# First MLP product: weights' high half with one 512-column moving operand instead of two of 256

## The chip, the cores and the metric

The kernel runs on one core of one Trainium2 chip. The metric is the device time of one execution in microseconds. Three runs of the kernel before have a median of 1898.04 us (1896.63 to 1898.8).

## What is computed

The reference is one layer of an encoder on x of 512 tokens by 2048 features, all in float32: a Conformer convolution module, then a squared-ReLU MLP, then a last RMSNorm.

```
h = rmsnorm(x, norm1_g)
u = h @ w_in + b_in;  val, gate = split(u)
u = causal_dwconv(val * sigmoid(gate), dw) + dw_b        # 31 taps
x = x + silu(layernorm(u, ln_g, ln_b)) @ w_out + b_out
x = x + square(relu(rmsnorm(x, norm2_g) @ mlp_w1)) @ mlp_w2   # 2048 -> 8192 -> 2048
out = rmsnorm(x, final_g)
```

## The kernel before

**Precision.** A float32 operand is kept as a high half (rounded to the matmul's fp32r type) and a low half (what is left). A product of two such operands is three matmuls into one PSUM tile: high by high, high by low, low by high. The helper `mm3` (L346 to L351) issues them: L349 multiplies the weights' high half wh with the input's high half, L350 wh with the input's low half, L351 the weights' low half wl with the input's high half. In the program's names the stationary operand (lhsT) is the weight, the moving one (rhs) the input.

**Stages.** First the convolution module runs, with its input product (to about 380 us) and its output product (L727 and L918, to about 590 us). Then comes the first MLP product, which is the stage that the change touches: a loop over 32 pairs of column blocks of mlp_w1 (`for n in range(NPAIR)`), from about 591 to 1247 us. Then comes the second MLP product (function `seven`) and the last norm.

**The first MLP product.** Each pair is a 2 by 2 block product by a scheme of seven products instead of eight, in the order FIRST: P1, P5, P6, P2, P7, P3, P4. An input factor of product x and row block p is the tile `y[p, x]`, 512 columns wide: its columns 0 to 255 (`t[:, :HT]`, HT = 256) are the high half of 256 tokens, columns 256 to 511 the low half. For each of the 8 row blocks p the loop calls `mm3`: three matmuls of 256 columns, 24 for a product, 168 for a pair, 5376 in all, all into the first 256 columns of a PSUM bank.

**Banks.** Four PSUM banks serve the loop. P1, P6, P7 and P4 accumulate one on the other in bank X, which alternates between two banks from pair to pair; P5 and P3 in bank Y; P2 in bank Z. After its last matmul each product's bank is read into a 256-column block of the pair's tile `four` (`READS`): P1, P5 and P6 by a ScalarE copy (L1037), P4 by a ScalarE relu (L1039), P2, P7 and P3 by a VectorE add to a block that an earlier product has filled (L1041). A product that goes on in a bank waits until the product before it there has been read.

**What runs beside it.** The weights of a product are made three products ahead (`stream.AHEAD = 3`, class `Early`): block differences on VectorE (L223), the cast to the high half on ScalarE (L212, L217), the low half on VectorE (L218) or GpSimd (L213). The pair before goes through class `Squares`, one step behind each product: relu (L964, three of the four blocks), square (L967), the high half (L973), sums and low halves on GpSimd (L978 to L981, L993), and stores to the buffer `spill` in memory, which the second product fetches (L953). The program is written out by hand here (`manual_schedule`): each engine works its instructions off in the order in which the code issues them. In the first pair the loop also holds the last of the residual (L868 to L873) and the last input factors y (L861, L862).

Of the kernel before, what the change touches and what calls it, by code (L numbers as in the profile page):

```python
# [14 lines left out]
AF = mybir.ActivationFunctionType  # L15
ALU = mybir.AluOpType
PSUM = bass.MemoryType.PSUM

P = 128
# [50 lines left out]
OPENS = ("P1", "P5", "P2")  # L70
# [14 lines left out]
HT = T // 2  # L85
# [3 lines left out]
def trunk(ctx: ExitStack, tc: tile.TileContext, xT, vec, fg, w_in, w_out, w1s, w2s, w2b, out):  # L89
    nc = tc.nc  # L90
# [21 lines left out]
    def bank(tag="mm"):  # L112
        return (psm if tag == "mm" else psx).tile([P, 512], F32, tag=tag, name=tag)
# [172 lines left out]
    def chunk():  # L286
        got = stream.get(cursor[0])
        cursor[0] += 1
        return got
# [56 lines left out]
    def mm3(ps, w, x, first, last, **how):  # L346

        (wh, wl), (xh, xl) = w, x
        nc.tensor.matmul(out=ps, lhsT=wh, rhs=xh, start=first, stop=False, **how)  # L349
        nc.tensor.matmul(out=ps, lhsT=wh, rhs=xl, start=False, stop=False, **how)  # L350
        nc.tensor.matmul(out=ps, lhsT=wl, rhs=xh, start=False, stop=last, **how)  # L351
# [6 lines left out]
    h = [None] * NT  # L358
# [494 lines left out]
    def pieces(p, products):  # L853
        for x in products:
            pool, tag, n = HOME[x]
            t = pool.tile([P, T], F32R, tag=tag, name="y", bufs=n)
            if x in ("P1", "P2", "P4"):
                f = parts[2 * p + (x != "P1")][:, first if x == "P4" else second]
            else:
                f = parts["s", p][{"P5": "s1", "P6": "s2", "P7": "s3", "P3": "s4"}[x]]  # L860
            nc.scalar.copy(out=t[:, :HT], in_=f)  # L861
            nc.vector.tensor_tensor(out=t[:, HT:], in0=f, in1=t[:, :HT].bitcast(F32), op=sub)  # L862
            y[p, x] = t

    def residual(n, b, pt):

        for i in range(4):
            nc.tensor.transpose(out=pt[:, i * P : (i + 1) * P], in_=xt[4 * n + i][:, b * P : (b + 1) * P], identity=ident)  # L868
        x2 = early.tile([P, 512], F32, tag="t", name="x2", bufs=4)
        nc.scalar.copy(out=x2, in_=pt)  # L870
        nc.scalar.dma_start(out=acc[b][n], in_=x2)
        sq = early.tile([P, 512], F32, tag="t", name="sq", bufs=4)
        nc.scalar.activation(out=sq, in_=pt, func=AF.Square, accum_out=ss[:, 4 * b + n : 4 * b + n + 1])  # L873
# [21 lines left out]
    with tc.manual_schedule():  # L895
        for n in range(4):
            evacuate(n, ps[n])
        for q in range(1, 4):
            ps = [bank() for _ in range(4)]
            stream.AHEAD = 3 if q < 3 else 2  # L900
            for c in range(8 if q < 3 else 6):
                w = chunk()
# [10 lines left out]
        for n in range(4):  # L913
            for k in range(12, NT):
                wh, wl = (x[:, k % 2 * 512 + n * P :][:, :P] for x in ends[k // 2 - 6])
# [31 lines left out]
        def fetch(n, sl=slice(0, 7 * HT)):  # L947

            i = n % SLOTS
            if n not in pairs:  # L950
                pairs[n] = tuple(slots[i].tile([P, 7 * HT], F32R, tag=f"{x}{i}", name=x, bufs=1) for x in ("ah", "al"))
            for h in range(2):
                nc.sync.dma_start(out=pairs[n][h][:, sl].bitcast(F32), in_=spill[n][:, h, sl])  # L953

        class Squares:
# [5 lines left out]
                self.block = dict(zip(("21", "11", "22", "12"), (self.a[:, i * HT : (i + 1) * HT] for i in range(4))))  # L961

            def relu(self):
                nc.scalar.activation(out=self.a[:, HT:], in_=self.a[:, HT:], func=AF.Relu)  # L964

            def square(self):
                nc.scalar.activation(out=self.a, in_=self.a, func=AF.Square)  # L967
# [53 lines left out]
        banks = {x: bank() for x in "0YZ1"}  # L1021
        before = None
        for n in range(NPAIR):
            now = None
            for i, product in enumerate(FIRST):
                w = chunk()
                where = {"X": str(n % 2)}.get(BANK[product], BANK[product])
                x = banks[where][:, :HT]
                for p in range(8):
                    t = y[p, product]  # L1030
                    sl = slice(p * P, (p + 1) * P)
                    mm3(x, tuple(h[:, sl] for h in w), (t[:, :HT], t[:, HT:]), product in OPENS and p == 0, p == 7, skip_group_check=True)
                if now is None:
                    now = Squares(n)
                to = now.block[READS[product]]
                if product in ("P1", "P5", "P6"):
                    nc.scalar.copy(out=to, in_=x)  # L1037
                elif product == "P4":
                    nc.scalar.activation(out=to, in_=x, func=AF.Relu)  # L1039
                else:  # L1040
                    nc.vector.tensor_tensor(out=to, in0=x, in1=to, op=ALU.add)  # L1041
                if before:
                    before.step(i)
                if n == 0:
                    if i < 2:
                        residual(3, 2 * i, banks["1"])
                        residual(3, 2 * i + 1, banks["Z"])
                    elif i == 2:
                        pieces(6, ("P7", "P3"))
                        pieces(7, ("P7", "P3"))  # L1050
                        gone.close()
                        stage = gone.enter_context(tc.tile_pool(name="stage", bufs=1, side="right", reuse_waits="tile"))
                    elif i == 3:
                        nc.vector.tensor_reduce(out=r2, in_=ss.rearrange("p (b n) -> p b n", n=4), axis=mybir.AxisListType.X, op=ALU.add)
                        nc.vector.tensor_scalar(out=r2, in0=r2, scalar1=1.0 / D, scalar2=RMS_EPS, op0=ALU.mult, op1=ALU.add)
                        nc.vector.reciprocal(out=r2, in_=r2)
                if n == NPAIR - 1:
                    if i == 3:
                        left.close()
                        slots += [ctx.enter_context(tc.tile_pool(name="slots", bufs=1, reuse_waits="tile"))] * 2  # L1060
                        slots += [late.enter_context(tc.tile_pool(name="slots2", bufs=1, reuse_waits="tile"))] * 2
                        for p in range(4):
                            fetch(p, slice(0, FORE))
                    elif i > 4:
                        for p in (2 * i - 10, 2 * i - 9):
                            fetch(p, slice(FORE, 7 * HT))
            before = now
# [72 lines left out]
    for q in range(2):  # L1140
        seven(NG - 1, q, 1)
        last_pair(LASTS + q)
        for n in (2 * q, 2 * q + 1):
            for m in range(4):
                raw = wts.tile([P, 1024], F32, tag="raw", name="raw", bufs=4)
                nc.sync.dma_start(out=raw[:, :512], in_=w2b[n, m])
                wh = lasts.tile([P, 512], F32R, tag=f"wh{n}{m}", name="w2h")
                wl = lasts.tile([P, 512], F32R, tag=f"wl{n}{m}", name="w2l")
# [6 lines left out]
    for i in range(2):  # L1155
        t = wts.tile([P, 1024], F32, tag="raw", name="fgt", bufs=4)
        nc.scalar.dma_start(out=t, in_=fg[i * 1024 : (i + 1) * 1024].partition_broadcast(P))
        fgt += [t[:, :512], t[:, 512:]]
    for b in range(NTOK):
# [6 lines left out]
        for i, cs in enumerate(pieces):  # L1166
# [3 lines left out]
            for kk in range(4):  # L1170
                ak = a[kk]
                wh, wl = wl2[kk][n]
# [64 lines left out]
```

## Time and profile before

| what | value |
|---|---|
| median of three runs | 1898.04 us |
| profiled execution | 1898.16 us |
| its span on the core | 1896.4 us |
| granted TensorE clock, mean | 0.988 |
| TensorE busy | 1838.8 us (97%) |
| VectorE / ScalarE / GpSimd busy | 1254.5 / 1138.0 / 1247.4 us |
| matmuls | 10866 |
| read from memory, written | 255.65 MB, 65.54 MB |

The engines carry short names in the profile: PE is TensorE's matmuls, PEld its weight loads, DVE VectorE, ACT ScalarE, POOL GpSimd, SP the queue that issues most loads. L349 is line 349 of the kernel. The matmuls of TensorE are pipelined: the duration in a row is longer than the time from one start to the next. The busy time of an engine counts no time twice.

### The profile page before, as it was taken

The page shows a single profiled execution, that of the slowest core. Times are in us where ns is not written, and L with a number is a line of the kernel's source. Part 1 is how long each engine was busy: PE and PEld are TensorE (multiplying, and loading weights), DVE is VectorE, ACT ScalarE, POOL GpSimd, SP SyncE. Part 2 cuts the span into 40 slices and gives each one's busy share as a digit, 9 for nine tenths or more (in the row PEclk, how much of TensorE's full clock was granted, in tenths as well). Part 3 has the DMA queues.
Part 4 walks back from the last instruction along what each step waited for, and adds up shares of the span by engine and source line. Part 5 has one row for each costly group of instructions (what it writes and reads, how often), then busy time and mean ns, then how long its engine had stood idle before and what let it go on. Part 6 is the DMA issues. An engine that isn't in the chain of part 4 may idle for free.

```text
span 1896.4 us, 29173 instructions
## 1 busy us (share of the span) xinstructions
PE 1838.8 (97%) x10866; PEld 1634.9 (86%) x10866; DVE 1254.5 (66%) x1997; ACT 1138.0 (60%) x1770; POOL 1247.4 (66%) x704
## 2 busy tenths in 40 slices
PE   6999999989998999999999999979999999999998
PEld 5888888978887999999999999957888888888876
DVE  8899999994338655555555555526666666666685
ACT  6444444456346666666666666646767776777663
POOL 5699999944433667767767767666566556665643
PEclk9999999999999999999999999989999999999999
DMA  5233333206333455655655655587746647556342
GB/s 213 91 97 96 100 122 100 78 1 220 114 121 122 161 198 186 210 194 181 216 193 179 221 193 179 198 319 275 277 134 232 235 148 271 187 172 237 99 145 100
DMA packets 93165, 323.08 MB, mean 170 GB/s; under 512 B 10336, under 2 KB 10976, under 8 KB 93024
## 3 DMA queue, kind: packets, MB, share of 16 engines
q1 hardware_dynamic: 72432, 258.76, 41.8%
q10 hardware_dynamic: 20592, 62.46, 8.2%
q8 instruction: 85, 1.39, 0.3%
q14 instruction: 56, 0.46, 0.1%
HBM read 255.65 MB, written 65.54 MB: 169 GB/s over the span
## 4 chain that ended last, share of the span: by engine, by line
PE 84%; DVE 7%; DMA 2%; ACT 2%; POOL 2%; issue 1%; SPq 0%; ACTq 0%; DVEq 0%; POOLq 0%
PE mm L350 26%; PE mm L351 26%; PE mm L349 26%; PE mm L727 7%; DVE ax L432 1%; POOL b L166 1%; POOL wl L187 1%; DMA xt<-in_xT 1%; DVE d L616 1%; DVE xl L343 1%; ACT ax L191 0%; DVE y L862 0%; DMA spill<-sl 0%; DVE d L694 0%; DMA acc<-x 0%
## 5 line engine op out<-in xcount | busy, mean ns | idle before, releaser
L349 PE MATMUL mm<-y,wh 128*128 128x256 f32 x1792 | 508.1, 284 | 2.6 <-ACT y L861 2.6
L350 PE MATMUL mm<-y,wh 128*128 128x256 f32 x1792 | 507.6, 283 | 0.1
L351 PE MATMUL mm<-y,wl 128*128 128x256 f32 x1792 | 507.5, 283 | 0.0
L166 POOL TENSOR_TENSOR b<-b,b 128x1024 f32<-128x1024 f32 x120 | 287.7, 2410 | 211.7 <-DMA b<-in_w2s 173.7
L213 POOL TENSOR_TENSOR wl<-b,wh 128x1024 fp32r<-128x1024 f32 x96 | 231.6, 2413 | 212.9 <-ACT wh L212 212.9
L349 PEld LDWEIGHTS mm<-y,wh 128*128 128x128 f32 x1792 | 344.5, 192 | 3.3 <-ACT y L861 2.8
L350 PEld LDWEIGHTS mm<-y,wh 128*128 128x128 f32 x1792 | 344.5, 192 | 0.3 <-DVE y L862 0.3
L351 PEld LDWEIGHTS mm<-y,wl 128*128 128x128 f32 x1792 | 344.4, 192 | 0.0
L350 PE MATMUL mm<-wl,ah 128*128 128x512 f32 x840 | 329.4, 392 | 12.7 <-DVE wl L192 7.9
L349 PE MATMUL mm<-wh,ah 128*128 128x512 f32 x840 | 328.2, 391 | 5.7 <-ACT wh L185 5.1
L351 PE MATMUL mm<-wh,al 128*128 128x512 f32 x840 | 328.5, 391 | 0.0
L192 DVE TENSOR_TENSOR wl<-b,ax 128x512 fp32r<-128x512 f32 x360 | 232.1, 683 | 136.8 <-ACT ax L191 103.8
L185 ACT CAST wh<-b 128x1024 fp32r<-128x1024 f32 x210 | 219.6, 1052 | 164.9 <-PE mm L351 145.0
L133 POOL TENSOR_TENSOR wl<-raw,wh 128x1024 fp32r<-128x1024 f32 x87 | 211.5, 2448 | 104.5 <-ACT wh L132 104.5
L1083 DVE SCALAR_TENSOR_TENSOR acc<-mm,shift,acc 128x512 f32<-128x512 f32 (+1 forms) x241 | 172.1, 745 | 99.2 <-PE mm L351 87.3
L432 DVE SCALAR_TENSOR_TENSOR ax<-u,v,ax 128x512 f32<-128x512 f32 x327 | 218.1, 751 | 0.0
L349 PE MATMUL mm<-xh,wh 128*128 128x512 f32 (+1 forms) x544 | 208.2, 383 | 5.1 <-ACT wh L132 5.1
L351 PE MATMUL mm<-xh,wl 128*128 128x512 f32 (+1 forms) x544 | 207.8, 382 | 3.4 <-DVE wl L133 3.4
L350 PE MATMUL mm<-xl,wh 128*128 128x512 f32 (+1 forms) x544 | 208.3, 383 | 1.3 <-DVE xl L343 1.3
L191 ACT COPY ax<-wh 128x512 f32<-128x512 f32 x360 | 200.3, 585 | 10.8 <-DVE wl L192 7.6
L350 PEld LDWEIGHTS mm<-wl,ah 128*128 128x128 f32 x840 | 158.4, 189 | 48.3 <-DVE wl L192 9.5
L349 PEld LDWEIGHTS mm<-wh,ah 128*128 128x128 f32 x840 | 158.0, 188 | 42.4 <-ACT wh L185 6.4
(203 smaller groups left out, 3021.1 us busy)
## 6 DMA issues: line engine op xcount, KB each, us to landing
b<-in_w1s SPq DMA_DIRECT2D x128, 512.0 KB, 5.0
b<-in_w2s SPq DMA_DIRECT2D x120, 512.0 KB, 4.1
raw<-in_w_in SPq DMA_DIRECT2D x63, 512.0 KB, 3.7
ah<-spill SPq DMA_DIRECT2D x26, 896.0 KB, 7.4
al<-spill SPq DMA_DIRECT2D x26, 896.0 KB, 9.2
raw<-in_w_out SPq DMA_DIRECT2D x32, 512.0 KB, 3.7
spill<-sh ACTq DMA_DIRECT2D x32, 512.0 KB, 7.4
spill<-sl ACTq DMA_DIRECT2D x32, 512.0 KB, 6.2
```

The source lines that it names most:

```text
L133: (nc.vector if sl.stop == cut else self.eng).tensor_tensor(out=lo[:, sl], in0=raw[:, sl], in1=hi[:, sl].bitcast(F32), op=ALU.subtract)
L166: nc.gpsimd.tensor_tensor(out=raw[to, hs], in0=raw[x, hs], in1=raw[y, hs], op=sub)
L185: nc.scalar.copy(out=hi, in_=s)
L191: nc.scalar.copy(out=st, in_=hi[:, sl].bitcast(F32))
L192: nc.vector.tensor_tensor(out=lo[:, sl], in0=s[:, sl], in1=st, op=sub)
L213: nc.gpsimd.tensor_tensor(out=lo, in0=raw[b], in1=hi.bitcast(F32), op=ALU.subtract)
L349: nc.tensor.matmul(out=ps, lhsT=wh, rhs=xh, start=first, stop=False, **how)
L350: nc.tensor.matmul(out=ps, lhsT=wh, rhs=xl, start=False, stop=False, **how)
L351: nc.tensor.matmul(out=ps, lhsT=wl, rhs=xh, start=False, stop=last, **how)
L432: nc.vector.scalar_tensor_tensor(out=o, in0=a, scalar=w, in1=c, op0=ALU.mult, op1=ALU.add)
L727: nc.tensor.matmul(out=ps[n][:, sl], lhsT=a[:, wsl], rhs=x[:, sl], start=first and a is wh and x is hi, stop=last and x is lo)
L1083: nc.vector.scalar_tensor_tensor(out=t, in0=ps, scalar=r2[:, b : b + 1], in1=t, op0=ALU.mult, op1=ALU.add)
```

## The change

Instead of `mm3` the loop issues two matmuls for each row block. The first takes the weights' high half against all 512 columns of the tile y, so that the bank's left half gets high by high and its right half high by low. The second takes the weights' low half against the 256 columns of the high half, into the left half. The bank then holds the product in two halves that are still to be added. So every product is read twice: P2, P7 and P3 by two VectorE adds into the block (L1039 and L1042 in the changed kernel), P1, P5, P6 and P4 by a ScalarE copy of the left half (L1041) and a VectorE add of the right half (L1042). P4 is no longer passed through relu when it is read; the relu of the step behind (L964) takes all four blocks, 1024 columns.

```
     def relu(self):
-        nc.scalar.activation(out=self.a[:, HT:], in_=self.a[:, HT:], func=AF.Relu)
+        nc.scalar.activation(out=self.a, in_=self.a, func=AF.Relu)
...
-    x = banks[where][:, :HT]
+    x = banks[where]
     for p in range(8):
         t = y[p, product]
-        sl = slice(p * P, (p + 1) * P)
-        mm3(x, tuple(h[:, sl] for h in w), (t[:, :HT], t[:, HT:]), product in OPENS and p == 0, p == 7, skip_group_check=True)
+        wh, wl = (h[:, p * P : (p + 1) * P] for h in w)
+        nc.tensor.matmul(out=x, lhsT=wh, rhs=t, start=product in OPENS and p == 0, stop=p == 7, skip_group_check=True)
+        nc.tensor.matmul(out=x[:, :HT], lhsT=wl, rhs=t[:, :HT], start=False, stop=p == 7, skip_group_check=True)
...
-    if product in ("P1", "P5", "P6"):
-        nc.scalar.copy(out=to, in_=x)
-    elif product == "P4":
-        nc.scalar.activation(out=to, in_=x, func=AF.Relu)
+    if product in ("P2", "P7", "P3"):
+        nc.vector.tensor_tensor(out=to, in0=x[:, :HT], in1=to, op=ALU.add)
     else:
-        nc.vector.tensor_tensor(out=to, in0=x, in1=to, op=ALU.add)
+        nc.scalar.copy(out=to, in_=x[:, :HT])
+    nc.vector.tensor_tensor(out=to, in0=x[:, HT:], in1=to, op=ALU.add)
```

The order of the instructions on VectorE shows where the new reads stand. In a pair of the loop, before, from the read of P3 (first row) over the end of the pair to the read of P2 of the next (last row); L223 and L218 prepare weights:

```order
L1041 TENSOR_TENSOR four<-mm,four 128x256
L218 TENSOR_TENSOR wl<-mm,wh 128x512 x2
L223 TENSOR_TENSOR ax<-mm,b_12851 128x512 x2
L218 TENSOR_TENSOR wl<-ax,wh 128x512 x2
L223 TENSOR_TENSOR mm<-b_12927,mm 128x512 x2
L218 TENSOR_TENSOR wl<-mm,wh 128x512 x2
L1041 TENSOR_TENSOR four<-mm,four 128x256
```

The same stretch of the changed kernel, from the two reads of P3 over P4, P1, P5 and P6 to the first read of P2:

```order
L1039 TENSOR_TENSOR four<-mm,four 128x256
L1042 TENSOR_TENSOR four<-mm,four 128x256
L218 TENSOR_TENSOR wl<-mm,wh 128x512 x2
L1042 TENSOR_TENSOR four<-mm,four 128x256
L223 TENSOR_TENSOR ax<-mm,b_11374 128x512 x2
L1042 TENSOR_TENSOR four<-mm,four 128x256
L218 TENSOR_TENSOR wl<-ax,wh 128x512 x2
L1042 TENSOR_TENSOR four<-mm,four 128x256
L223 TENSOR_TENSOR mm<-b_11436,mm 128x512 x2
L1042 TENSOR_TENSOR four<-mm,four 128x256
L218 TENSOR_TENSOR wl<-mm,wh 128x512 x2
L1039 TENSOR_TENSOR four<-mm,four 128x256
```

Where the passes on weights followed one another, a read of a bank now stands between any two of them.

On VectorE in the first pair, before, from the last input factors to the read of P7 (the last row); the three rows on `shift` are the small passes of the second norm:

```order
L862 TENSOR_TENSOR y<-ysums,y 128x256 x4
L218 TENSOR_TENSOR wl<-mm,wh 128x512 x2
L1041 TENSOR_TENSOR four<-mm,four 128x256
L1054 TENSOR_REDUCE shift<-shift 128x4
L1055 TENSOR_SCALAR shift<-shift 128x4
L1056 RECIPROCAL shift<-shift 128x4
L223 TENSOR_TENSOR ax<-mm,b_5362 128x512 x2
L1041 TENSOR_TENSOR four<-mm,four 128x256
```

And in the changed kernel, where the first row is the new read of P6:

```order
L1042 TENSOR_TENSOR four<-mm,four 128x256
L862 TENSOR_TENSOR y<-ysums,y 128x256 x4
L218 TENSOR_TENSOR wl<-mm,wh 128x512 x2
L1039 TENSOR_TENSOR four<-mm,four 128x256
L1042 TENSOR_TENSOR four<-mm,four 128x256
L1055 TENSOR_REDUCE shift<-shift 128x4
L1056 TENSOR_SCALAR shift<-shift 128x4
L1057 RECIPROCAL shift<-shift 128x4
L223 TENSOR_TENSOR ax<-mm,b_5355 128x512 x2
L1039 TENSOR_TENSOR four<-mm,four 128x256
L1042 TENSOR_TENSOR four<-mm,four 128x256
```

Three reads more stand there ahead of the end of P7's read: P6's, and the second ones of P2 and P7.

## Rows read from the trace of the kernel before

**Rows 1.** The page, busy us (share of the span) x instructions of each engine.
```profile
PE 1838.8 (97%) x10866; PEld 1634.9 (86%) x10866; DVE 1254.5 (66%) x1997; ACT 1138.0 (60%) x1770; POOL 1247.4 (66%) x704
```
**Rows 2.** The page, the chain that ended last, by engine.
```profile
PE 84%; DVE 7%; DMA 2%; ACT 2%; POOL 2%; issue 1%; SPq 0%; ACTq 0%; DVEq 0%; POOLq 0%
```
**Rows 3.** Three stretches: us, busy PE, PEld, DVE, ACT, POOL, clock, DMA share, GB/s.
```profile
465.17:497.84 32.67, 32.67 (x146) 27.04 (x145) 12.44 (x11) 11.20 (x18) 14.36 (x6) 1.00 0.38 118
700.00:1200.00 500.00, 500.00 (x4169) 500.00 (x4168) 276.19 (x470) 322.46 (x522) 351.37 (x224) 1.00 0.58 198
1400.00:1600.00 200.00, 200.00 (x882) 165.30 (x882) 129.98 (x202) 144.65 (x203) 119.43 (x50) 1.00 0.64 222
```
**Rows 4.** ScalarE in order of time, two reads of P4: start, us, instruction [idle before].
```profile
904.48 0.38 ACT L1039 ACTIVATE four<-mm 128x256 f32<-128x256 f32 x1 [1.92 <-PE mm L351]
...
924.64 0.38 ACT L1039 ACTIVATE four<-mm 128x256 f32<-128x256 f32 x1 [1.92 <-PE mm L351]
```
**Rows 5.** The chain in order of time, output product: start, us, what.
```profile
464.30 0.87 PE ax L868 x8
465.17 32.67 PE mm L727 x144
```
**Rows 6.** Groups by line and form: shapes, count | busy us, mean ns | idle before.
```profile
L1041 DVE TENSOR_TENSOR four<-mm,four 128x256 f32<-128x256 f32 x96 | 40.6, 423 | 2.7
...
L967 ACT ACTIVATE four<-four 128x1024 f32<-128x1024 f32 x32 | 34.0, 1062 | 0.0
...
L964 ACT ACTIVATE four<-four 128x768 f32<-128x768 f32 x32 | 27.1, 848 | 0.0
```
**Rows 7.** VectorE in order of time, from P2's to P3's read of one pair.
```profile
917.49 1.30 DVE L223 TENSOR_TENSOR ax<-mm,b 128x512 f32<-128x512 f32 x2 [1.07 <-ACT mm L228]
918.88 0.42 DVE L1041 TENSOR_TENSOR four<-mm,four 128x256 f32<-128x256 f32 x1
...
921.92 0.42 DVE L1041 TENSOR_TENSOR four<-mm,four 128x256 f32<-128x256 f32 x1
```
**Rows 8.** VectorE in order of time, first pair.
```profile
611.77 3.16 DVE L862 TENSOR_TENSOR y<-ysums,y 128x256 fp32r<-128x256 f32 x4 [3.22 <-ACT y L861]
614.85 1.28 DVE L218 TENSOR_TENSOR wl<-mm,wh 128x512 fp32r<-128x512 f32 x2
616.05 0.41 DVE L1041 TENSOR_TENSOR four<-mm,four 128x256 f32<-128x256 f32 x1
...
617.35 1.28 DVE L223 TENSOR_TENSOR ax<-mm,b 128x512 f32<-128x512 f32 x2
618.54 0.41 DVE L1041 TENSOR_TENSOR four<-mm,four 128x256 f32<-128x256 f32 x1
```
**Rows 9.** TensorE in order of time, first pair, end of P3 and start of P4.
```profile
618.76 0.28 PE L350 MATMUL mm<-y,wh 128*128 128x256 f32 x1
618.88 0.28 PE L351 MATMUL mm<-y,wl 128*128 128x256 f32 x1
619.10 0.36 PE L349 MATMUL mm<-y,wh 128*128 128x256 f32 x1
```
**Rows 10.** TensorE's waits from 585 to 640 us: total us, times, longest us.
```profile
PE mm L868 <- ACT sq L873: 3.9, 2, 3.0
```
**Rows 11.** GpSimd in order of time, last pair, first and last of eight passes.
```profile
1235.14 2.41 POOL L213 TENSOR_TENSOR wl<-b,wh 128x1024 fp32r<-128x1024 f32 x1 [4.14 <-ACT wh L212]
...
1251.95 2.39 POOL L993 TENSOR_TENSOR sl<-four,sh 128x1024 fp32r<-128x1024 f32 x1
```
**Rows 12.** The chain in order of time, behind the first MLP product.
```profile
1251.95 2.40 POOL sl L993
1254.36 7.59 DMA spill<-sl
1263.81 0.79 SPq L1079
```
**Rows 13.** ScalarE in order of time, high half of the last pair.
```profile
1249.44 1.05 ACT L973 CAST sh<-four 128x1024 fp32r<-128x1024 f32 x1
```

## The prediction

> **What bounds the kernel now.** I read the page first. TensorE is busy 97% of the span, VectorE and GpSimd 66%, ScalarE 60% [rows 1], and 84% of the chain that ended last is TensorE [rows 2]. Then the table by stretch, which shows what bounds the stage that is changed [rows 3]. From 700 to 1200 us, inside the loop over the 32 pairs, TensorE has work in 500.00 of 500 us at a granted clock of 1.00, the 2.4 GHz level, and starts 4169 matmuls: 119.9 ns each. VectorE is busy 276, ScalarE 322 and GpSimd 351 us there, the DMA engines 58%. So TensorE waits for nothing in the loop, and a pair lasts as long as its 168 matmuls. The rows of one pair say the same: the pass that reads the last product starts at 904.48 and one pair later at 924.64 [rows 4], 20.16 us or 120.0 ns for each of 168.
>
> A page's duration of a matmul is of no use for a sum, since the matmuls overlap. What one costs is the step from start to start, and I need it for two widths. At 256 columns it is the 120.0 ns above. At 512 columns the first stage's output product gives 144 matmuls in 32.67 us, 226.9 ns [rows 5], and the second MLP product 882 in 200 us, 226.8 ns [rows 3]. 256 columns more cost 106.9 ns, which is 256 columns at 2.4 GHz (106.7 ns), so **either width carries the same 13.3 ns** beside its columns.
>
> **The change part by part.** *TensorE.* For each of 8 row blocks of each of 7 products of each pair (56 a pair, 1792 in all), three matmuls of 256 columns become one of 512 and one of 256. The columns stay (768), one matmul less is issued, and its weight load with it. Before: 3 x 120.0 = 360.0 ns. After: 226.9 + 120.0 = 346.9 ns. Saved: 13.1 ns, 0.734 us a pair (20.16 to 19.43), 23.5 us in 32 pairs. No row of before has the two widths in turn. Bounds: nothing saved, if 512 columns cost two steps of 256 here (240 ns); and 13.1 ns, because in no steady stretch, of either width, does a matmul cost less than its columns and 13.3. I take the upper end, since every row of either width gives it.
>
> The weight load could be the limit behind 256 columns: eight matmuls of 128 columns take 0.87 us [rows 5], 109 ns each, twice their columns, so about 109 ns is what a load allows, just under 120.0. After the change each 512-wide matmul still has its load under one of 256, exactly as now, and the other load gets more room. The sum stands whichever of load and columns makes the 120.0.
>
> The Trainium skill, "TensorE: Matmul & The Clock Gate", section "Back-to-back issue gap", gives N/2.4 + 2.5 ns for the step of a matmul by itself. By that the removed matmul is worth 2.5 ns, 4.5 us in all (an estimate from that page), which speaks against this change. The steps of 120.0 and 226.9 ns here lie 10.8 ns above it at both widths, and the measured ones are used.
>
> *VectorE and ScalarE.* Each product's bank now has two halves to be read. P1, P5, P6, P4 get an add behind ScalarE's copy, P2, P7, P3 a second add: 7 a pair at 423 ns [rows 6], 3.0 us. VectorE goes from 276/500 x 20.16 = 11.1 us a pair to 14.1 of 19.43, 73%. ScalarE's relu takes 1024 columns for 768, 1062 for 848 ns [rows 6]: 13.0 to 13.2 us, 68%. Both lie beside TensorE's work. But the queues are in order, and VectorE now stops at the end of each of the seven products where it stopped at three. Behind it are the weights' preparation, which runs three products (8.3 us) ahead, and the next use of the bank. Bank X is used by every second product, so its adds have one product (2.78 us). The fullest place is P7 and P3: VectorE reads P7 at 918.88, then makes four passes on weights and reads P3 at 921.92 [rows 7]. P7 ended at 904.4 + 5 x 2.88 = 918.8, P3 at 921.7: at once, and 0.2 us late. P2's second add (0.34 from start to start) falls into the 1.07 us in which VectorE waits for ScalarE before 917.49 [rows 7], so P7 is still read at once and released 0.8 us after its end, 2 us early. P3 is read 0.2 + 0.34 + 0.1 = 0.65 late and released 1.4 us after its end; its bank Y is wanted two products later. I cost all this at nothing in pairs 1 to 31. If that cover were gone, TensorE would wait before P4 in every pair (the slower rival below).
>
> *The first pair* is such a place. It shares VectorE with the rest of the input factors: from 611.77 to 618.95 it works without a pause (four passes to y, two on weights, P2's add, three small ones, two on weights, P7's add) [rows 8], and P4, which needs P7's bank, starts 0.22 us after the matmul before it instead of 0.12, at 619.10 [rows 9]. It waited 0.1 us for that add. Now the second adds of P2 and P7 and some 0.13 us of P6's new add come before it: 0.34 + 0.34 + 0.13 = 0.8, and P4 starts at 619.9. What P6, P2, P7 and P3 save is lost in that wait, P4 saves its own 0.1, and the pair **costs 0.7 us**. P1 and P5 gain nothing, since TensorE waits 3.9 us for ScalarE's passes on the residual behind them [rows 10].
>
> *The end of the loop.* From P5 of the last pair on GpSimd is the chain: eight passes without a pause from 1235.14 to 1254.34 [rows 11], the first of them waiting for ScalarE's cast behind P5's copy. What ends them is the low half of the last pair, and then come its store to spill of 7.59 us [rows 12] and the loads behind that. So what the five products after P5 save brings nothing (5 x 0.105 = 0.5 us). The last pair's reads must still be in time for GpSimd's last pass at 1251.95: ScalarE's high half starts at 1249.44 and takes 1.05 [rows 13], 1.45 us early. The new add (0.45) and the wider relu (0.2) delay it by 0.65, P4's earlier end gives 0.5 back: covered, by 1.3 us. Past that it would go straight to the end.
>
> **Sum:** -0.7 for pair 0, 30 x 0.734 = 22.0 for pairs 1 to 30, 2 x 0.105 = 0.2 for the last: 21.5 us. All behind moves up whole, since the second MLP product is again TensorE's (200.00 of 200 us from 1400 on [rows 3]). The profiled execution took 1898.16 us, 0.12 over the median of the three runs: 1876.7, and against the median **1876.5 us**.
>
> **The rivals.** *The cost goes with the columns, not with the matmul.* If one pass of 512 in this loop costs two of 256, 360 ns stay, and the first pair loses what its adds cost: 1898.0 + 0.8 = 1898.8 us. For it: no row of before alternates widths. Against it: the same 13.3 ns at both widths, in three stages. Chance 0.04. By the 2.5 ns of the Trainium skill's page above (an estimate) it would be some 1894 us; the chance covers that too.
>
> *VectorE becomes late in every pair: slower.* The mechanism is the first pair's: P4 waits for P7's second add. It decides from the point where that bank is released over 2.78 us after P7's end, and makes the pair longer than now where the wait passes 0.73 us. Were it as in pair 0 (0.1 now, 0.8 more, and 0.4 that the four products before P4 save: 1.3 us), a pair would last 20.7 us, 0.57 more than now, 31 pairs 17.6, with pair 0 18 us: 1916 us. For it: VectorE's seven stops, and the one pair where it does happen. Against: outside that pair VectorE has 5 us a pair free, and the release comes 2 us early. Chance 0.03.
>
> *Half of the gain is given back at the change of stage.* Behind the last low half come the store, fetches and loads on SP's queue [rows 12]. If these, and not their releases, set when the second product gets going, they do not move up whole, and some 10 us go: 1887 us. For it: from 1200 to 1400 us TensorE does wait. Against: the transfers are issued behind releases that move up with TensorE, and the loop's DMA share only rises from 58 to 60%. Chance 0.07.
>
> **How the numbers follow.** The forecast, 0.86, has a range of its own from 1874.5 (nothing lost in pair 0 and at the end, 23.5 saved) to 1880 (a second wait of the first pair's size, and 2 us more at the change of stage). The range over all cases adds a little on either side: 1874 to 1881.5. Under 0.2% (3.8 us) a change cannot be told from none. Faster: the forecast and the half gain, 0.93. Same: the first rival, 0.04. Slower: 0.03.
>
> **What would show it.** Right: in the loop 112 matmuls a pair, steps of 227 and 120 ns in turn, the read of P4 every 19.43 us, TensorE without a pause from pair 1 on; VectorE near 73%; a wait of over 1 us before P4 of the first pair; GpSimd without a pause from the last P5 to the last low half. Wrong: another step than 120 ns behind the 256-wide matmul, waits of TensorE for VectorE's adds in later pairs, or a second product that starts by other than 21.5 us earlier.

## The result and the profile after

The changed kernel has a median of 1881.19 us in six executions, the kernel before 1898.2 in six; the ratio is 0.9906 with an interval of 0.988 to 0.9933. The direction is the forecast one and 1881.2 lies in the range, near its upper end: 17.0 us are gained for 21.5 predicted. The six executions do not lie together, though: two at 1872.6 and 1874.2, four from 1881.0 to 1886.4, where the kernel before keeps within 2.7 us. Three executions of kernels further below, at 2028 us (granted clock 0.84), 3878 and 4851 us (1.00), are left out of every ratio and median here. The profiled execution is the one of 1872.64 us (span 1870.8). So the first trace shows the gain whole, and the question for the experiments is where the other executions lose some 11 us of it.

The same kinds of row in the profile after, the stretches with the columns of [rows 3]:

```profile
PE 1813.1 (97%) x9074; PEld 1536.4 (82%) x9074; DVE 1343.4 (72%) x2221; ACT 1147.0 (61%) x1770; POOL 1249.2 (67%) x704
```

```profile
465.17:497.84 32.67, 32.54 (x144) 26.61 (x144) 13.60 (x13) 11.48 (x18) 14.36 (x6) 1.00 0.39 128
700.00:1200.00 500.00, 500.00 (x2887) 440.88 (x2886) 359.85 (x669) 343.96 (x543) 365.53 (x233) 1.00 0.59 202
1400.00:1600.00 200.00, 200.00 (x883) 165.43 (x882) 127.10 (x197) 140.97 (x196) 128.90 (x54) 1.00 0.58 208
```

1792 matmuls fewer; in the loop TensorE is still without a pause at a granted clock of 1.00, now with 2887 starts in 500 us, 173.2 ns each, 346.4 ns for a wide and a narrow one (predicted 346.9). A stretch's count takes in the matmuls under way at its edges, so that such a pace comes out some 0.3 ns low: the start times in the trace give 346.7. VectorE is at 72% (73), ScalarE at 69% (68). The waits of TensorE from 585 to 1300 us, with the columns of [rows 10], name VectorE's new add once, for 0.5 us, and that is the first pair:

```profile
PE mm L350 <- DVE wl L192: 6.1, 2, 5.5
PE mm L350 <- POOL wl L187: 4.0, 2, 2.5
PE mm L868 <- ACT sq L873: 3.9, 2, 2.9
PE mm L349 <- ACT wh L185: 3.4, 2, 2.4
PE mm L1033 <- DVE y L862: 3.1, 1, 3.1
PE mm L1033 <- DVE four L1042: 0.5, 1, 0.5
```

Where this execution's 25.6 us of span come from can be read off ScalarE's reads of the banks (least, median and longest ns, first and last start). Before, the first started at 602.0 and the last at 1247.2 us:

```profile
L1037 ACT COPY four<-mm x96: 368/373/396, 602.0 to 1235.7; 128x256 f32<-128x256 f32 x96
...
L1039 ACT ACTIVATE four<-mm x32: 384/384/385, 622.2 to 1247.2; 128x256 f32<-128x256 f32 x32
```

After, one group has them all:

```profile
L1041 ACT COPY four<-mm x128: 373/374/396, 600.9 to 1223.4; 128x256 f32<-128x256 f32 x128
```

The loop takes 622.5 us for 645.2, 22.7 less. The code ahead of it, which is the same, took 1.1 less in this execution, and what comes behind it took 647.4 us (1870.8 - 1223.4) for 649.2.

### The profile page after: what moved, and what is told of

Read it like the earlier page. It is cut to its first block, busy times and chain, and to the rows that moved or that the text cites. A ratio compares the mean times of both kernels' runs of the same rounds, so it can differ in the third digit from the quotient of the medians.

```text
span 1870.8 us, 25813 instructions
## 1 busy us (share of the span) xinstructions
PE 1813.1 (97%) x9074; PEld 1536.4 (82%) x9074; DVE 1343.4 (72%) x2221; ACT 1147.0 (61%) x1770; POOL 1249.2 (67%) x704
## 4 chain that ended last, share of the span: by engine, by line
PE 80%; DVE 10%; ACT 3%; POOL 2%; DMA 2%; issue 2%; SPq 0%; ACTq 0%; DVEq 0%; POOLq 0%
PE mm L1033 21%; PE mm L350 13%; PE mm L351 13%; PE mm L349 13%; PE mm L1034 11%; PE mm L727 7%; DVE ax L432 4%; POOL b L166 1%; POOL wl L187 1%; DVE xl L343 1%; DVE d L616 1%; DVE y L862 0%; ACT ax L191 0%; ACT wh L185 0%; DVE u L390 0%
## 5 line engine op out<-in xcount | busy, mean ns | idle before, releaser
L1033 PE MATMUL mm<-y,wh 128*128 128x512 f32 x1792 | 623.2, 392 | 3.7 <-DVE y L862 3.1
L1034 PE MATMUL mm<-y,wl 128*128 128x256 f32 x1792 | 502.2, 280 | 0.0
L1033 PEld LDWEIGHTS mm<-y,wh 128*128 128x128 f32 x1792 | 335.7, 187 | 78.6 <-DVE y L862 3.4
L1034 PEld LDWEIGHTS mm<-y,wl 128*128 128x128 f32 x1792 | 339.1, 189 | 0.0
L191 ACT COPY ax<-wh 128x512 f32<-128x512 f32 x360 | 200.4, 586 | 10.8 <-DVE wl L192 7.5
L351 PEld LDWEIGHTS mm<-wh,al 128*128 128x128 f32 x840 | 158.7, 189 | 33.1
L132 ACT CAST wh<-raw 128x1024 fp32r<-128x1024 f32 (+1 forms) x93 | 94.9, 1037 | 112.3 <-PE mm L350 68.5
```

The lines of the kernel that those rows point to most:

```text
L191: nc.scalar.copy(out=st, in_=hi[:, sl].bitcast(F32))
L1033: nc.tensor.matmul(out=x, lhsT=wh, rhs=t, start=product in OPENS and p == 0, stop=p == 7, skip_group_check=True)
L1034: nc.tensor.matmul(out=x[:, :HT], lhsT=wl, rhs=t[:, :HT], start=False, stop=p == 7, skip_group_check=True)
```

## The experiments

**The change twice more, the reads alone and the matmuls alone.** `after_again` and `after_look` are the changed kernel unaltered. In `narrow_two_reads` the wide matmul is cut in two, with the bank's halves and both reads kept:

```
-    nc.tensor.matmul(out=x, lhsT=wh, rhs=t, ...)
+    nc.tensor.matmul(out=x[:, :HT], lhsT=wh, rhs=t[:, :HT], ...)
+    nc.tensor.matmul(out=x[:, HT:], lhsT=wh, rhs=t[:, HT:], ...)
```

In `wide_one_read` the add of the right half is taken out:

```
-    nc.vector.tensor_tensor(out=to, in0=x[:, HT:], in1=to, op=ALU.add)
```

> The changed kernel once more, unaltered. Its six executions lie between 1872.6 and 1886.4 us, where the kernel before keeps within 2.7 us. Theory L (the loop): in a longer execution TensorE waits in the loop of the first MLP product; a pair lasts over 19.43 us, 0.3 us more in each for 10 us in all. Theory S (the change of stage): the loop is at 19.43 us a pair in every execution, and a longer one restarts later behind it, or waits inside the second product. If the profiled execution is again near 1873, it tells nothing on this; the times then show only how often the long ones come.

> Three matmuls of 256 columns for each row block, as before the change, but with the two halves and both reads of the change: the reads alone. If the matmul that the change drops carries 13.3 ns, this kernel loses the whole gain: pairs of 20.16 us, and the time of the kernel before plus the first pair's 0.8, about 1899 us. Rival (the reads give some of the gain, by relu's place or another order): clearly under 1898. Of the spread: if it comes from the reads (theory R), the executions of this kernel spread by over 5 us too; if it comes from the shorter pair (theory P), they keep within 3 us.

> The change's two matmuls, but of each bank only the left half is read (the product of the weights' high half with the input's low half is left out of the result): the matmuls alone. Forecast 23 to 25 us under the kernel before (23.5 from the step, no loss in the first pair), 1873 to 1876 us. If the spread comes from the reads (theory R), this kernel keeps within 3 us; if it comes from the shorter pair (theory P), it spreads by over 5.

> The changed kernel unaltered, for one more profiled execution. Theories L and S as with the repetition above: in an execution of over 1880 us, L has pairs of over 19.6 us, S has pairs of 19.43 us and a second product that starts or ends late.

`narrow_two_reads` gains nothing that is clear of the noise: a median of 1895.26 us in eleven executions against 1898.53 (about 1899 was expected), ratio 0.9991 (0.998 to 1.0001). Its loop starts the matmuls of before, 4169 in 500 us, with VectorE at 346 us of them:

```profile
700.00:1200.00 500.00, 500.00 (x4169) 500.00 (x4168) 345.97 (x644) 329.28 (x523) 350.87 (x225) 1.00 0.58 196
```

So the gain is the dropped matmul's, and the added reads cost nothing that can be measured in the times. The test by spread (theory R over 5 us, P within 3) decided nothing: these eleven spread over 9.3 us, but the kernel before spreads over 8.7 us on this chip too. Here the spread goes with the mean granted clock: the six executions up to 1895.3 us have 0.990 or 0.991, the five from 1897.9 on 0.986 to 0.989. `wide_one_read` has 0.992 (0.9897 to 0.9943), the changed kernel beside it 0.9919 (0.9897 to 0.9941): without the added reads it is no better. It also has the two groups, 1874.5 and 1875.7 us against 1884.4 to 1888.7. The changed kernel's were 1871.3 and 1873.0 against 1883.1 to 1888.0, and 1871.4 in `after_look`. The added reads are out as a cause of the groups; what is left is the matmuls or the shorter pair. My 1873 to 1876 for `wide_one_read` holds for the lower group alone. The three profiled executions with wide matmuls were all in the lower group and showed nothing on L or S.

**Half of the pairs.** The change in pairs 0 to 15 alone, or in pairs 16 to 31 alone; the others get `mm3` and one read.

```
+    wide = n < NPAIR // 2          # last_half_wide: n >= NPAIR // 2
```

> The change for pairs 0 to 15 alone; pairs 16 to 31 as before the change (relu over all four blocks throughout). Profiled: 0.5 x 23.5 less the first pair, about 11 us under the kernel before, near 1887 us. The timed executions of the change lie in two groups, 1873 to 1876 and 1881 to 1889 us, and every profiled one in the lower. Theory L (the longer executions lose their 10 to 12 us in the loop, where pairs are wide): the upper group lies 5 to 6 us over the lower here. Theory S (they lose it at the change of stage, behind the last pairs, or in the second product): here the last pairs are as before, so the executions keep within the spread of the kernel before (1893.7 to 1902.3, 8.7 us), around 1887, with no upper group.

> The change for pairs 16 to 31 alone; pairs 0 to 15 as before the change. Profiled: 16 x 0.734 = 11.7 us less what the end of the loop keeps, near 1886.5 us. Theory L: an upper group 5 to 6 us over the lower, as with the first half. Theory S: the whole 10 to 12 us between two groups, since the last pairs and the change of stage are as in the changed kernel.

Measured: 1890.03 us (1885.3 to 1892.4) and 1890.22 (1888.7 to 1890.7), ratios 0.9956 and 0.9955, some 8 us gained by either half, and the profiled executions, at 1892.4 and 1890.7 us, lie well over the 1887 and 1886.5 that were expected of them. No execution of the second half shows the 10 to 12 us that S puts at the end, and the times alone do not separate two groups. The traces do. In the stretches with wide matmuls the first half and the second half start these, again with the columns of [rows 3]:

```profile
700.00:900.00 200.00, 200.00 (x1134) 173.50 (x1133) 141.46 (x266) 133.91 (x212) 144.09 (x92) 1.00 0.59 200
```

```profile
950.00:1200.00 250.00, 250.00 (x1417) 216.97 (x1416) 176.60 (x330) 168.50 (x267) 179.01 (x115) 1.00 0.57 195
```

200 / 1134 is 176.4 ns and 250 / 1417 is 176.4 ns, for 173.2 in the changed kernel's first trace, with TensorE busy throughout and the clock at 1.00. Two matmuls take 353 ns for 346.4, which is why both profiled executions fell short of the expectation. That is neither a wait in the loop nor one behind it: the step itself has two values. 6.6 ns in 32 x 56 places is 11.8 us, near the distance of the two groups (11.2 us between the means of all executions below).

**The order of the widths.** If the extra hangs on the change from one width to the other, equal widths side by side should be rid of it. `grouped_by_8` issues a product's eight wide matmuls and then its eight narrow ones, `grouped_by_2` two and two:

```
-    for p in range(8):
-        ... wide(p); narrow(p)
+    for q in range(0, 8, 2):                       # grouped_by_8: one group of 8
+        for p in range(q, q + 2): ... wide(p)
+        for p in range(q, q + 2): ... narrow(p)
```

> The changed kernel with the two widths apart: of each product first its eight matmuls of 512 columns, then its eight of 256, 14 changes of width a pair instead of 112. Known so far: in the profiled executions of the change 16 wide and 16 narrow starts take 346.4 ns a pair of them, in those of the two half kernels 353, and 32 x 56 x 6.6 ns is 11.8 us, the distance of the two groups of times. Theory W (the extra 6.6 ns hangs on a narrow matmul that follows a wide one, or the reverse): it comes here 7 times a pair for 56, at most 1.5 us in all, so all executions lie near the lower group, 1871 to 1877 us, median near 1873.5. Theory M (in a longer execution each 512-wide matmul of this loop takes 6.6 ns more, whatever follows): the two groups stay, most executions at 1881 to 1888.

> Two wide, two narrow, in turn: 56 changes of width a pair. Theory W: an upper group 6 us over the lower (about 1878 to 1881 for 1872 to 1875). Theory M: as the changed kernel, 1881 to 1888 in most executions.

> The changed kernel unaltered, on the same chip as the two kernels that group the widths. Two groups again: some executions at 1871 to 1876, most at 1881 to 1888 us, median 1881 to 1884.

Measured: `grouped_by_8` 1876.0, 1876.4 and 1879.4 us, ratio 0.9889 (0.9874 to 0.9903); `grouped_by_2` 1874.5 to 1876.4, ratio 0.9878 (0.9863 to 0.9892); the changed kernel beside them 1872.4 to 1874.5 four times, 1884.5 and 1887.0. M falls: the wide matmuls are there, and none of the seven executions is long. W does not hold as I stated it either, since it asked for an upper group 6 us up in `grouped_by_2`, and there is none. Nor does grouping by eight come down to the pace of the short executions, as W would have it, and one of its three lies over W's 1871 to 1877. The loops of `grouped_by_8` and `grouped_by_2` read:

```profile
700.00:1200.00 500.00, 500.00 (x2865) 440.04 (x2864) 354.91 (x664) 338.32 (x540) 360.83 (x230) 1.00 0.59 201
```

```profile
700.00:1200.00 500.00, 500.00 (x2873) 436.28 (x2872) 357.92 (x665) 341.46 (x540) 363.08 (x231) 1.00 0.60 202
```

That is 349.0 and 348.1 ns for a wide and a narrow matmul.

**Once more, and another order.** `turned` keeps each row block's two matmuls together, but turns them in every other block: wide, narrow, narrow, wide.

```
+    pair = [(x, wh, t, ...), (x[:, :HT], wl, t[:, :HT], False)]
+    for o, l, r, st in pair if p % 2 == 0 else pair[::-1]:
+        nc.tensor.matmul(out=o, lhsT=l, rhs=r, start=st, ...)
```

> Two wide, two narrow, in turn, once more. Its four executions lay at 1874.5 to 1876.4 us, five of six of the change beside it at 1872 to 1875 or 1884 to 1887. Theory A (only wide and narrow singly in turn has the second cadence of 353 ns): again every execution at 1873 to 1878, none over 1880. Theory M (an execution is long whatever the order of the widths): some of the executions over 1880.

> The change's matmuls in the order wide, narrow, narrow, wide, wide, narrow and so on: as with the grouping by two no width stands alone, but each row block's two matmuls stay together, as in the change. Theory A: every execution at 1873 to 1878. Rival (the second cadence hangs on the weights of one row block being used one behind the other): groups as in the change, some at 1881 to 1888.

> The changed kernel unaltered beside the two, on the same chip: two groups, 1871 to 1876 and 1881 to 1888 us, of the 15 timed executions so far 10 in the upper.

Measured: `grouped_by_2` again 1873.8 to 1877.1 us, ratio 0.9869 (0.9855 to 0.9883), `turned` 1874.1, 1875.3 and 1877.0, ratio 0.9873 (0.9859 to 0.9888): as theory A has it, and the rival on the row block's weights falls. The changed kernel lay at 1870.0 to 1875.2 three times and at 1882.4 to 1885.6 three times, and this time the profiled execution was a long one, 1885.62 us (span 1883.8). Its loop:

```profile
700.00:1200.00 500.00, 500.00 (x2832) 433.55 (x2830) 352.94 (x660) 334.51 (x529) 358.49 (x227) 1.00 0.59 201
```

```profile
L1041 ACT COPY four<-mm x128: 372/373/398, 604.0 to 1238.1; 128x256 f32<-128x256 f32 x128
```

2832 starts in 500 us are 176.6 ns each, 353.1 for the two, with no wait of TensorE from 640 to 1230 us, the same clock, and VectorE and ScalarE with less to do per us. The loop lasts 634.1 us, 11.6 more than in the short execution. In order of time (start, us, instruction), the long execution first, then the short one:

```profile
999.78 0.40 PE L1033 MATMUL mm<-y,wh 128*128 128x512 f32 x1
1000.02 0.28 PE L1034 MATMUL mm<-y,wl 128*128 128x256 f32 x1
1000.14 0.40 PE L1033 MATMUL mm<-y,wh 128*128 128x512 f32 x1
...
1001.20 0.40 PE L1033 MATMUL mm<-y,wh 128*128 128x512 f32 x1
```

```profile
999.95 0.39 PE L1033 MATMUL mm<-y,wh 128*128 128x512 f32 x1
1000.18 0.28 PE L1034 MATMUL mm<-y,wl 128*128 128x256 f32 x1
1000.30 0.39 PE L1033 MATMUL mm<-y,wh 128*128 128x512 f32 x1
...
1000.99 0.39 PE L1033 MATMUL mm<-y,wh 128*128 128x512 f32 x1
```

Above, four wide and four narrow ones take 1.42 us, below three and three 1.04: 355 and 347 ns for the two, as far as two decimals go. It is not something that comes and goes: of the stretches of 100 us from 640, 760, 880, 1000 and 1120 us each has 567 to 569 starts in the long execution and 578 or 579 in the short one.

In all the changed kernel ran 25 times: 12 executions at 1870.0 to 1875.2 us, 13 at 1881.0 to 1888.0, none between. (The last expectation miscounts: before it 10 of 19 had been long.) The mean granted clock does not sort them, 0.987 to 0.991 in the short ones and 0.986 to 0.992 in the long ones. The three kernels with equal widths side by side have 14 executions in the comparisons, 1873.8 to 1879.4.

## Why the prediction was right, and which term was off

*TensorE's step.* The mechanism was right: the gain is the dropped matmul's, in the loop, as `narrow_two_reads` shows by gaining nothing clear of the noise. Its weight load went with it, and no run tells the two apart. The term "Saved: 13.1 ns, 0.734 us a pair" holds in the 12 short ones of the 25 executions (13.6 ns from 346.4, in the four of them that have a trace). In the other 13, of which one has a trace, the two widths in turn take 353.1 ns, so that 6.9 ns are saved, 0.39 us a pair. The step that was off is "The sum stands whichever of load and columns makes the 120.0": two steps, each measured in a stream of its own width, were added as if the order of widths did not matter. The bound was right to ask for it ("No row of before has the two widths in turn"), but I took the upper end and gave the lower one a chance of 0.04.

Even where the sum holds, its parts do not. The prediction named "another step than 120 ns behind the 256-wide matmul" as a sign of being wrong, and it is there in every trace of the changed kernel. The means of the start times from 700 to 1200 us are 230.0 ns behind a wide matmul and 116.7 behind a narrow one in the first trace, 231.8 and 114.8 in that of `after_again`, and 236.4 and 117.0 in the long execution's. So 346.9 was met by two steps that are off in opposite directions, and most of what a long execution adds stands behind the wide matmul.

*The number.* That the median fell into the range is partly luck. No execution of the changed kernel lies at the forecast of 1876.5 us, which is in the gap between the groups. The median of 1881.19 us, 4.7 us over the forecast, is the mean of the two shortest of four long executions, 1880.98 and 1881.4. In the three later comparisons the changed kernel's median was 1883.4, 1873.95 and 1878.77 us, two of them outside 1874 to 1881.5.

*The formula.* The Trainium skill's N/2.4 + 2.5 ns ("TensorE: Matmul & The Clock Gate", "Back-to-back issue gap"), which that page gives for a matmul by itself, would make the two 325.0 ns (an estimate from that page); no run here comes near it, neither 346.4 nor 353.1. The steps of the kernel before lie 10.8 and 11.1 ns above it, not 10.8 at both widths.

*VectorE and ScalarE.* Costed at nothing, and nothing it was: no wait of TensorE for the adds after the first pair in either trace. The slower rival did not come about.

*The first pair.* The place was right, the size smaller. TensorE waits there for P7's second add:

```profile
617.73 0.28 PE L1034 MATMUL mm<-y,wl 128*128 128x256 f32 x1
618.54 0.47 PE L1033 MATMUL mm<-y,wh 128*128 128x512 f32 x1 [0.53 <-DVE four L1042]
```

VectorE runs through from 610.79 to 618.39, with these rows at P2 and P7, the counterparts of [rows 8]:

```profile
615.03 0.41 DVE L1039 TENSOR_TENSOR four<-mm,four 128x256 f32<-128x256 f32 x1
615.47 0.42 DVE L1042 TENSOR_TENSOR four<-mm,four 128x256 f32<-128x256 f32 x1
...
616.00 0.20 DVE L1056 TENSOR_SCALAR shift<-shift 128x4 f32<-128x4 f32 x1
...
617.52 0.41 DVE L1039 TENSOR_TENSOR four<-mm,four 128x256 f32<-128x256 f32 x1
617.97 0.42 DVE L1042 TENSOR_TENSOR four<-mm,four 128x256 f32<-128x256 f32 x1
```

P4 starts 17.64 us after the loop's first read (618.54 - 600.9) for 17.10 before: 0.54 later, where I had 0.8. The second reads cost 0.44 each, not 0.34, since a second add to the same block starts 0.45 after the first; the small pass at 616.00 took 0.20 us where it took 0.65 before, which gave that back and more.

*The end of the loop.* It came as predicted. GpSimd's eight passes and ScalarE's last high half, counterparts of [rows 11] and [rows 13]:

```profile
1211.88 2.42 POOL L213 TENSOR_TENSOR wl<-b,wh 128x1024 fp32r<-128x1024 f32 x1 [3.58 <-ACT wh L212]
...
1228.73 2.40 POOL L993 TENSOR_TENSOR sl<-four,sh 128x1024 fp32r<-128x1024 f32 x1
```

```profile
1226.45 1.05 ACT L973 CAST sh<-four 128x1024 fp32r<-128x1024 f32 x1
```

The last pass starts 16.85 us after the first, before 16.81: what the last five products save does bring nothing. The last high half ends at 1227.50, 1.2 us early (1.3 predicted). Behind that the store in the chain takes 5.79 us in this execution, where [rows 12] has 7.59. That the part behind the loop is also 1.8 us shorter in all does not make the store its cause: the last low half starts 5.3 us after the last read of a bank, 4.8 before, and the rest is shorter too.

```profile
1228.73 2.41 POOL sl L993
1231.16 5.79 DMA spill<-sl
1236.96 0.32 SPq L953
```

So the rival by which half of the gain is given back at the change of stage came near the time and was wrong in the place: the long execution that has a trace loses it in the loop, and behind the loop it takes 645.7 us (1883.8 - 1238.1), less than the short one.

**A version without the long executions.** `grouped_by_2` has 0.9878 and 0.9869 against the kernel before, in two comparisons, with no long execution; the changed kernel beside it had 0.989 and 0.9889. Its medians were 1875.19 and 1875.1 us, for 1873.95 and 1878.77. It keeps the gain of the short executions nearly whole: 2873 starts in 500 us, 348.1 ns for the two widths, for 346.4. The intervals overlap (0.9863 to 0.9892 and 0.9866 to 0.9913), so it is not shown to be the faster; that its eight executions lie within 3.4 us is what it has ahead.

## What to carry to other kernels

Cost a removed matmul by steps from start to start, and take them from a stream in which the widths follow each other as they will; steps of two pure streams need not add up. When the executions of a kernel fall into two groups, count the starts in equal stretches of a trace of each before looking for a wait: here TensorE waited for nothing in the loop of either and the clock was the same. Where adds are put behind a loop's bound engine, look for the place at which their engine has no pause: here they cost something only there.

## What the runs showed of the hardware that was not expected

Long streams of one width have one pace in every trace: 120.0 ns at 256 columns, 226.9 at 512 (226.7 to 227.0 in the second product from 1400 to 1600 us, by the start times). Eight are too few for that: in `grouped_by_8` wide matmuls side by side start 230.6 ns apart on average, the first two steps of the eight being 233.3 and 235.8 ns and the last three behind a wide matmul 226.7. A wide and a narrow matmul strictly in turn have two, 346.4 and 353.1 ns for the two, and in the traces an execution keeps one of them through the loop. The difference, 6.7 ns, is 16 cycles at 2.4 GHz, and 120.0, 226.9, 346.4 and 353.1 are 18, 34, 52 and 53 times that within 0.3 ns. With two of a width side by side it was 348 ns in all three profiled executions, which is no such multiple. What sets the pace of an execution stays open: the same program took either on each chip on which it ran more than once, and no experiment here touched what differs at its start. With equal widths side by side none of 14 executions was long, where 13 of 25 were with the two strictly in turn; why the order does this is not shown.
